# Two-layer trunk on one core: all block sums of the MLPs to VectorE, and their second-half products spread between tiles of the first half

## Chip, cores, metric

One core of a Trainium2 chip. The metric is device time of one execution in microseconds (us); several executions are taken and the median is compared. Engines are named as the profile names them: PE is TensorE (PEld its weight loads), DVE is VectorE, ACT is ScalarE, POOL is GpSimd, SP is SyncE, which here only issues DMAs.

## What is computed

Two layers on 512 tokens of width 1024, all in fp32. Layer 0 mixes tokens by Mamba-2 SSD, layer 1 by HGRN2; each mixer is followed by a layer norm, an MLP of hidden width 4096, a second layer norm and a gated embedding. Cut to the part that is touched:

```python
def sq_relu_mlp(h, w1, w2):
    a = jax.nn.relu(h @ w1)          # [512, 1024] x [1024, 4096]
    return (a * a) @ w2              # [512, 4096] x [4096, 1024]

for i in range(2):
    mix = ssd_mixer(...) if i % 2 == 0 else hgrn2_mixer(...)
    h = layer_norm(ALPHA * x + mix, ...)
    h = layer_norm(ALPHA * h + sq_relu_mlp(h, mlp_w1[i], mlp_w2[i]), ...)
    x = h + sigmoid(h @ ple_w_gate[i]) * (p[i] @ ple_w_proj[i])
```

## The kernel before

**Split products.** Every matrix is held as two halves of fp32r, a rounded one ("hi") and the rest ("lo"), and each product is three matmuls: hi·hi, hi·lo, lo·hi (`mm3`, L116, L117, L118). A weight buffer of 128x1024 comes by one SP DMA of 512 KB into a ring of three (`raws`, L103), ACT casts it to `whi` (L110), DVE subtracts to get `wlo` (L112); the rings of `whi` and `wlo` have five buffers each. This pair of instructions runs for every weight buffer of the kernel, and it is asked for ahead of its use by a priority (`LEAD`).

**First half of an MLP.** A tile is one weight buffer against all tokens: 24 matmuls of 128x512 (rows `pj<-b,whi`). ACT applies Relu and, for two tiles together, Square. Four tiles make a quarter of a hidden group of 8 (`hidden(g, p)`: group g = 0..3, half p = 0, 1). `half_blocks` then makes the seven left operands of a 2x2 Strassen-Winograd product: a11, a12, a22 and four sums s1..s4. Each is split by `put`: ACT cast (L263), DVE subtract (L264). The four sums are POOL instructions (L269 to L275). Operands s3 and s4 lie in the pool `blk` (2 buffers) and the other five in `b8` (9 buffers).

**Second half.** `block_product` of a group is seven products instead of eight: p1 (a11), p2 (a12), p6 (s2), p7 (s3), p5 (s1), p4 (a22), p3 (s4). A product is two halves c = 0, 1 of 12 matmuls, each half into a PSUM bank; at its end DVE adds the bank to `acc` (L314, or L316 for the first group). p1, p6, p5 and p3 all use the same two banks, py0 and py1, one for each c, and keep adding in them: p6's half c can start only when DVE has read p1's half c. The right operands are four weight blocks of two buffers each, and four sums of them, t1..t4: eight buffers come by SP into a ring `r` of ten, and eight POOL instructions make the sums (L290 t1, L292 t2, L321 t3, L325 t4).

**Order.** A scheduler places the instructions of each engine in the order in which they are written, moved forward by the priorities (`LEAD` 100, `SUMS` 220 places). `ORDER` lists quarters of the first half (h, group, half) and whole block products (o): `h00 h01 h10 o0 h11 h20 o1 h21 h30 h31 o2 o3`. So the last two block products of an MLP, 14 products in a row, have no first-half tile between them. In the last one the order of products is p1, p2, p6, p5, p3, then the norm of chunks 0 and 1 (`after`), p7, p4, then chunks 2 and 3.

**Norm.** `norm` takes `acc` by four chunks of 128 tokens: statistics (L189, L191), root (L193), reciprocal (L195), two scalings (L196, L197), and then for each half of the chunk four transpositions on PE (L206) into one bank `pt`, an ACT cast (L209) and a DVE subtract (L210). The norm ahead of the MLP runs between the matmuls of the mixer's output projection and the MLP's first matmuls.

Of the kernel before, what the change touches and what calls it, by code (L numbers as in the profile page):

```python
# [15 lines left out]
P = 128  # L16
T = 512
# [13 lines left out]
ORDER = "h00 h01 h10 o0 h11 h20 o1 h21 h30 h31 o2 o3".split()  # L31
SUMS = 220
# [10 lines left out]
def trunk(ctx: ExitStack, tc, a):  # L43
# [9 lines left out]
    sm = pool("sm", 2)  # L53
    psj = pool("psj", 4, space=PSUM)
# [17 lines left out]
    mlp = dict(r=10, blk=2, sg=2)  # L72
# [67 lines left out]

    begin("ssd")
# [114 lines left out]
    def half_blocks(blk, z0, z1, p):  # L256
# [20 lines left out]

    def block_product(w, blk, first, after=None):


        with tc.high_priority(offset=SUMS):
            raw = {}
            for i, j in ((0, 0), (0, 1), (1, 1), (1, 0)):
                raw[i, j] = []
                for u in range(2):
                    raw[i, j].append(tmp("r", [P, 1024]))
                    nc.sync.dma_start(raw[i, j][u], w[i][j][u])
            t1, t2, t3, t4 = raw[0, 1], [tmp("r", [P, 1024]) for _ in range(2)], raw[0, 0], raw[1, 0]
            for u in range(2):
                nc.gpsimd.tensor_sub(t1[u], raw[0, 1][u], raw[0, 0][u])  # L290
            for u in range(2):
                nc.gpsimd.tensor_sub(t2[u], raw[1, 1][u], t1[u])  # L292
# [3 lines left out]
        def product(x, f, name, start, i, j, then=None):  # L296
            us = [split(v) for v in f]
            if then is not None:
                with tc.high_priority(offset=LEAD):
                    then()  # L300
# [18 lines left out]
        def sums3():  # L319
            for u in range(2):  # L320
                nc.gpsimd.tensor_sub(t3[u], t2[u], raw[0, 0][u])  # L321

        def sums4():
            for u in range(2):
                nc.gpsimd.tensor_sub(t4[u], raw[1, 0][u], t2[u])  # L325

        product("a11", raw[0, 0], "x", True, 0, 0, sums3)
# [6 lines left out]
        if after is None:  # L334
            for f in (p7, p5, p4, p3):
                f()
        else:
            p5(), p3(), after(0), after(1)
            p7(), p4(), after(2), after(3)
# [700 lines left out]
```

## Time and profile before

| | us |
|---|---|
| median of 3 runs (lowest to highest) | 1508.86 (1508.42 to 1509.92) |
| the profiled execution | 1508.68 |
| its span in the trace | 1506.9 |
| PE busy | 1470.1 (98%) |
| DVE busy | 1101.0 (73%) |
| ACT busy | 723.5 (48%) |
| POOL busy | 274.8 (18%) |
| moved by DMA | 149.93 MB, mean 99 GB/s |

Busy time is the sum over the engine's instructions; matmuls overlap, so PE's busy time is not PE at its peak. "Granted clock" is the share of TensorE's full clock in a stretch. In rows of the trace the columns are start, duration, engine, line, operation, output<-inputs, shapes, and in brackets the idle time before the instruction and what ended it. MLP 0 spans about 401 to 727 us of the profiled span, MLP 1 about 1110 to 1436 us.

### The profile page before, as it was taken

To read this page: it belongs to the slowest core of one execution; us is meant where nothing else is said; L and a number is where in the kernel's file an instruction comes from. 1 tells how busy PE (TensorE), PEld (TensorE's weight loads), DVE (VectorE), ACT (ScalarE), POOL (GpSimd) and SP (SyncE) were. 2 spreads that over 40 slices of the span, in tenths; PEclk is the share of its full clock that TensorE was granted. 3 is DMA by queue.
4 is the path that set the end of the run, shared out by engine and by line. 5 is a ranking of instruction groups with operands and counts; after the bars stand their busy time and mean duration, and the time that the engine had idled before them with its cause. 6 is when DMAs were issued, how large, how long until landed. Compare 5 with 4: busy or idle time off the path is not lost.

```text
span 1506.9 us, 19584 instructions
## 1 busy us (share of the span) xinstructions
PE 1470.1 (98%) x7720; PEld 1222.1 (81%) x7720; DVE 1101.0 (73%) x1544; ACT 723.5 (48%) x1020; POOL 274.8 (18%) x136
## 2 busy tenths in 40 slices
PE   8999999999999999998999999999999999999898
PEld 5888888888888888876778998988798888887677
DVE  7998686787777586398944866769766958549883
ACT  6776455563364454453534453543245454444342
POOL 0000000001145251363000000000215435235200
PEclk9999999999999999998999999999999999999999
DMA  6433323234223324130223212222431423314022
GB/s 247 155 112 107 112 93 109 99 118 175 88 69 112 112 89 137 55 126 28 81 70 112 94 61 71 72 70 84 154 112 43 134 90 112 127 42 140 14 85 70
DMA packets 41612, 149.93 MB, mean 99 GB/s; under 512 B 4624, under 2 KB 5136, under 8 KB 41392
## 3 DMA queue, kind: packets, MB, share of 16 engines
q1 hardware_dynamic: 41520, 148.67, 29.4%
q8 instruction: 61, 1.00, 0.3%
q14 instruction: 31, 0.25, 0.1%
HBM read 146.49 MB, written 2.16 MB: 99 GB/s over the span
## 4 chain that ended last, share of the span: by engine, by line
PE 88%; DVE 9%; DMA 2%; ACT 1%; issue 0%; POOL 0%; SPq 0%; ACTq 0%; DVEq 0%
PE pj L116 23%; PE pj L117 23%; PE pj L118 23%; DVE wlo L112 4%; PE py L116 3%; PE py L118 3%; PE py L117 3%; DVE b L264 2%; PE py L778 1%; PE py L587 1%; DVE acc L314 1%; PE pm L557 1%; PE pt L206 1%; PE py L592 1%; DMA a<-in_pT 1%; DVE blk L264 1%
## 5 line engine op out<-in xcount | busy, mean ns | idle before, releaser
L116 PE MATMUL pj<-b,whi 128*128 128x512 f32 (+1 forms) x1024 | 392.0, 383 | 1.2 <-ACT whi L110 1.2
L118 PE MATMUL pj<-b,wlo 128*128 128x512 f32 (+1 forms) x1024 | 388.1, 379 | 0.0
L117 PE MATMUL pj<-b,whi 128*128 128x512 f32 (+1 forms) x1024 | 387.5, 379 | 0.0
L112 DVE TENSOR_TENSOR wlo<-raw,whi 128x1024 fp32r<-128x1024 f32 x180 | 230.4, 1281 | 110.5 <-ACT whi L110 109.6
L110 ACT CAST whi<-raw 128x1024 fp32r<-128x1024 f32 x180 | 188.8, 1050 | 237.3 <-PE pj L117 129.5
L112 DVE TENSOR_TENSOR wlo<-r,whi 128x1024 fp32r<-128x1024 f32 x112 | 194.0, 1737 | 89.7 <-ACT whi L110 89.7
L116 PE MATMUL pj<-whi,b 128*128 128x512 f32 (+1 forms) x712 | 252.3, 355 | 0.5 <-ACT sg L410 0.5
L117 PE MATMUL pj<-wlo,b 128*128 128x512 f32 (+1 forms) x712 | 249.6, 351 | 0.8 <-DVE wlo L112 0.8
L118 PE MATMUL pj<-whi,b 128*128 128x512 f32 (+1 forms) x712 | 250.1, 351 | 0.0
L116 PEld LDWEIGHTS pj<-b,whi 128*128 128x128 f32 x1024 | 192.9, 188 | 36.7 <-ACT whi L110 2.9
L118 PEld LDWEIGHTS pj<-b,wlo 128*128 128x128 f32 x1024 | 192.7, 188 | 35.9 <-DVE wlo L112 1.3
L117 PEld LDWEIGHTS pj<-b,whi 128*128 128x128 f32 x1024 | 192.9, 188 | 34.0 <-issue 1.9
L110 ACT CAST whi<-r 128x1024 fp32r<-128x1024 f32 x112 | 116.8, 1048 | 189.6 <-PE pj L117 60.9
L290 POOL TENSOR_TENSOR r<-r,r 128x1024 f32<-128x1024 f32 x16 | 45.1, 2826 | 767.6 <-DMA r<-in_w 760.0
L117 PEld LDWEIGHTS pj<-wlo,b 128*128 128x128 f32 x712 | 134.7, 189 | 18.4 <-DVE wlo L112 2.0
L116 PEld LDWEIGHTS pj<-whi,b 128*128 128x128 f32 x712 | 134.7, 189 | 17.7 <-ACT sg L410 0.7
L118 PEld LDWEIGHTS pj<-whi,b 128*128 128x128 f32 x712 | 134.5, 189 | 17.0 <-issue 0.2
L116 PE MATMUL py<-whi,b 128*128 128x512 f32 x192 | 77.2, 402 | 15.5 <-DVE acc L314 15.5
L118 PE MATMUL py<-whi,b 128*128 128x512 f32 x224 | 88.8, 398 | 0.0
L264 DVE TENSOR_TENSOR b<-b,b 128x512 fp32r<-128x512 f32 x48 | 62.7, 1322 | 21.5 <-ACT b L263 21.3
L117 PE MATMUL py<-wlo,b 128*128 128x512 f32 x192 | 76.6, 399 | 0.6 <-DVE wlo L112 0.6
L321 POOL TENSOR_TENSOR r<-r,r 128x1024 f32<-128x1024 f32 x16 | 39.8, 2485 | 125.0 <-DVE wlo L112 125.0
(217 smaller groups left out, 2064.3 us busy)
## 6 DMA issues: line engine op xcount, KB each, us to landing
raw<-in_w SPq DMA_DIRECT2D x64, 512.0 KB, 3.6
r<-in_w SPq DMA_DIRECT2D x64, 512.0 KB, 3.7
raw<-in_wssd SPq DMA_DIRECT2D x40, 512.0 KB, 3.6
a<-csd SPq DMA_DIRECT2D x16, 512.0 KB, 3.9
raw<-in_wso SPq DMA_DIRECT2D x16, 512.0 KB, 3.5
raw<-in_wg SPq DMA_DIRECT2D x16, 512.0 KB, 3.6
raw<-in_whvg SPq DMA_DIRECT2D x16, 512.0 KB, 3.5
raw<-in_whq SPq DMA_DIRECT2D x16, 512.0 KB, 3.6
```

The source lines that it names most:

```text
L110: nc.scalar.copy(hi[:, :n], f)
L112: nc.vector.tensor_sub(lo[:, :n], f, f32(hi[:, :n]))
L116: nc.tensor.matmul(out, sh, mh, start=start, stop=False, **kw)
L117: nc.tensor.matmul(out, sh, ml, start=False, stop=False, **kw)
L118: nc.tensor.matmul(out, sl, mh, start=False, stop=stop, **kw)
L206: nc.tensor.transpose(pt[:, j * P : (j + 1) * P], src[:, k * P : (k + 1) * P], ident)
L264: nc.vector.tensor_sub(lo, f, f32(hi))
L290: nc.gpsimd.tensor_sub(t1[u], raw[0, 1][u], raw[0, 0][u])
L314: nc.vector.tensor_add(d, ps, d)
L321: nc.gpsimd.tensor_sub(t3[u], t2[u], raw[0, 0][u])
L557: nc.tensor.matmul(pst_[:, c * P : (c + 1) * P], btok[:, c, :], xw[:, c].rearrange("p h q -> p (h q)"), start=True, stop=True)
L587: nc.tensor.matmul(yd[64 * r : 64 * r + 64, sl], xdt[:, 2 * c + r, :], m[:, r, sl], start=True, stop=True)
```

## The change

All sums go to DVE and are written into the buffer of one of their operands: block sums in `half_blocks` into the activation tiles, weight sums in a new function `weight_sums` into the load buffers. The weight blocks of p1, p2 and p3, which are no sums, are loaded again through the common ring `raws` (`unit` in place of `split`), 6 buffers a group, 48 DMAs of 512 KB in all, so that the ring `r` may be overwritten; `r` has 8 buffers instead of 10. `SUMS` is 300 places instead of 220. The order of the `put`s in `half_blocks` is another. Both `hidden` and `block_product` become generators that stop after each tile (T) and each product (Q), and `PERIODS` interleaves them: eight tiles, then three times fifteen steps in which products of one group alternate with tiles of the next, then the last group's seven products. A tile of 64 bytes per partition is allocated ahead of the phases' pools, which shifts their addresses by 64 bytes.

```diff
-ORDER = "h00 h01 h10 o0 h11 h20 o1 h21 h30 h31 o2 o3".split()
-SUMS = 220
+PERIODS = ("TTTTTTTT",) + 3 * ("TTQTQTQTQTQTQTQ",) + ("QQQQQQQ",)
+SUMS = 300
...
+    pad = pool("pad", 1)
...
-    mlp = dict(r=10, blk=2, sg=2)
+    mlp = dict(r=8, blk=2, sg=2)
...
+    nc.gpsimd.memset(mk(pad, [P, 16], "pad"), 0.0)
...
+        put("a11", a11)
         put("a22", a22)
-        put("a11", a11)
+        nc.vector.tensor_add(a22, a21, a22)
         put("a12", a12)
-        nc.gpsimd.tensor_add(a22, a21, a22)
+        nc.vector.tensor_sub(a21, a11, a21)
+        nc.vector.tensor_sub(a11, a22, a11)
+        nc.vector.tensor_sub(a12, a12, a11)
+        put("s2", a11)
+        put("s3", a21)
         put("s1", a22)
-        nc.gpsimd.tensor_sub(a21, a11, a21)
-        put("s3", a21)
-        nc.gpsimd.tensor_sub(a11, a22, a11)
-        put("s2", a11)
-        nc.gpsimd.tensor_sub(a12, a12, a11)
         put("s4", a12)
...
+    def weight_sums(w):
+
+        t = [[None, None] for _ in range(4)]
+
+        def load(i, u, src):
+            t[i][u] = tmp("r", [P, 1024])
+            nc.sync.dma_start(t[i][u], src)
+
+        with tc.high_priority(offset=SUMS):
+            for u in range(2):
+                load(0, u, w[0][1][u])
+                load(2, u, w[1][1][u])
+                nc.vector.tensor_sub(t[2][u], t[2][u], t[0][u])
+                load(1, u, w[0][0][u])
+                nc.vector.tensor_sub(t[0][u], t[0][u], t[1][u])
+                nc.vector.tensor_add(t[1][u], t[2][u], t[1][u])
+            for u in range(2):
+                load(3, u, w[1][0][u])
+                nc.vector.tensor_sub(t[3][u], t[3][u], t[1][u])
+        return t
...
-            us = [split(v) for v in f]
+            us = [split(v) if f in (t1, t2, t3, t4) else unit(v) for v in f]
...
+        for f in (p1, p2, p6, p5, p3, p7, p4) if after else (p1, p2, p6, p7, p5, p4, p3):
+            f()
+            if after and f is p3:
+                after(0), after(1)
+            if after and f is p4:
+                after(2), after(3)
+            yield
...
+        for g, period in enumerate(PERIODS):
+            if g < 4:
+                tiles = hidden(g)
+            if g > 0:
+                if g == 4:
+                    h_s, after = norm(2 * layer + 1)
+                w = [[[w2[8 * g - 8 + 4 * i + 2 * j + u] for u in range(2)] for j in range(2)] for i in range(2)]
+                products = block_product(w, blocks.pop(g - 1), g == 1, after if g == 4 else None)
+            for op in period:
+                next(tiles if op == "T" else products)
```

Line numbers move with the edit: matmuls from L116-L118 to L117-L119, `whi` and `wlo` from L110 and L112 to L111 and L113, the statistics from L189 and L191 to L191 and L193, the scalings from L196 and L197 to L198 and L199, the norm's subtract from L210 to L212, the addition to `acc` from L314 to L323. In the rows below a name's number is the kernel's own count.

**First place: the start of MLP 0's last group.** DVE's rows before. These rows end products of the group ahead (`py_878` and `py_877` are the shared banks, `pj_5362` and `pj_5363` those of p4) and split the last group's first buffers.

```order
L314 TENSOR_TENSOR acc_94<-py_878_5255,acc_94 128x512
L112 TENSOR_TENSOR wlo_5524<-r_5500,whi_5522 128x1024
L314 TENSOR_TENSOR acc_94<-pj_5362,acc_94 128x512
L112 TENSOR_TENSOR wlo_5528<-r_5502,whi_5526 128x1024
L314 TENSOR_TENSOR acc_94<-pj_5363,acc_94 128x512
L112 TENSOR_TENSOR wlo_5562<-r_5512,whi_5560 128x1024
L314 TENSOR_TENSOR acc_94<-py_877_5254,acc_94 128x512
L112 TENSOR_TENSOR wlo_5566<-r_5514,whi_5564 128x1024
```

POOL's rows before, the weight sums of that last group: t1, t2, then t3 written into the buffers `r_5500` and `r_5502` that two of the DVE rows above read, and t4 into `r_5512` and `r_5514` that the other two read.

```order
L290 TENSOR_TENSOR r_5504<-r_5504,r_5500 128x1024
L290 TENSOR_TENSOR r_5506<-r_5506,r_5502 128x1024
L292 TENSOR_TENSOR r_5516<-r_5508,r_5504 128x1024
L292 TENSOR_TENSOR r_5517<-r_5510,r_5506 128x1024
L321 TENSOR_TENSOR r_5500<-r_5516,r_5500 128x1024
L321 TENSOR_TENSOR r_5502<-r_5517,r_5502 128x1024
L325 TENSOR_TENSOR r_5512<-r_5512,r_5516 128x1024
L325 TENSOR_TENSOR r_5514<-r_5514,r_5517 128x1024
```

DVE's rows now at the same place. `py_860` is the last bank of the group ahead, `py_940` and `py_941` are p1's halves c = 0 and 1 of the last group, `pj_5611` is p2's first half. POOL has nothing left here.

```order
L323 TENSOR_TENSOR acc_99<-py_860_5050,acc_99 128x512
L323 TENSOR_TENSOR acc_99<-py_940_5571,acc_99 128x512
L113 TENSOR_TENSOR wlo_5645<-r_5549,whi_5643 128x1024
L323 TENSOR_TENSOR acc_99<-pj_5611,acc_99 128x512
L191 BN_STATS lnst_5745<-acc_99 128x6
L113 TENSOR_TENSOR wlo_5675<-r_5535,whi_5673 128x1024
L113 TENSOR_TENSOR wlo_5679<-r_5544,whi_5677 128x1024
L113 TENSOR_TENSOR wlo_5711<-raw_5707,whi_5709 128x1024
L323 TENSOR_TENSOR acc_99<-py_941_5572,acc_99 128x512
```

The weight sums of this group stand earlier in DVE's row now, and the addition that frees p1's second bank stands behind three `wlo` rows.

PE's rows before, the end of p1's first half (`py_927`) and the beginning of its second (`py_928`); `pj_5570` is p2's first half.

```order
L116 MATMUL py_927_5532<-whi_5526,b_820_4915 128x512
L117 MATMUL py_927_5532<-wlo_5528,b_820_4915 128x512
L118 MATMUL py_927_5532<-whi_5526,b_820_4915 128x512
L116 MATMUL pj_5570<-whi_5560,b_821_4916 128x512
L116 MATMUL py_928_5533<-whi_5522,b_820_4915 128x512
L117 MATMUL py_928_5533<-wlo_5524,b_820_4915 128x512
L118 MATMUL py_928_5533<-whi_5522,b_820_4915 128x512
```

PE's rows now: `py_941` is p1's second half, `pj_5612` the second half of p2, `py_940` the first half of p6.

```order
L117 MATMUL pj_5612<-whi_5607,b_830_4941 128x512
L117 MATMUL py_941_5572<-whi_5561,b_829_4940 128x512
L118 MATMUL py_941_5572<-wlo_5563,b_829_4940 128x512
...
L119 MATMUL py_941_5572<-whi_5567,b_829_4940 128x512
L118 MATMUL pj_5612<-wlo_5609,b_830_4941 128x512
L119 MATMUL pj_5612<-whi_5607,b_830_4941 128x512
L117 MATMUL py_940_5571<-whi_5639,b_833_4944 128x512
```

p1's second half stood ahead of all but one matmul of p2 and now stands behind 22 of p2's 24, two matmuls ahead of p6's first half.

**Second place: the last chunk of the norm ahead of MLP 0.** DVE's rows before, from the second statistics to the first subtract of the transposed half.

```order
L189 BN_STATS lnst_3329<-acc_94 128x6 x2
L112 TENSOR_TENSOR wlo_3617<-raw_3613,whi_3615 128x1024
L191 BN_AGGR lnmv_3332<-lnst_3329 128x2
L196 SCALAR_TENSOR_TENSOR acc_94<-acc_94,lnmv_3332,a_3098 128x1024
L195 RECIPROCAL lnrs_3336<-lnsd_3334 128x1
L197 SCALAR_TENSOR_TENSOR acc_94<-acc_94,lnrs_3336,b_3099 128x1024
L210 TENSOR_TENSOR b_555_3104<-pt_3340,b_553_3102 128x4x128
```

DVE's rows now; rows L292 to L298 are weight sums of group 0.

```order
L191 BN_STATS lnst_3334<-acc_99 128x6 x2
L292 TENSOR_TENSOR r_3850<-r_3850,r_3848 128x1024
L212 TENSOR_TENSOR b_557_3110<-pt_3299,b_555_3108 128x4x128
L193 BN_AGGR lnmv_3337<-lnst_3334 128x2
L294 TENSOR_TENSOR r_3848<-r_3848,r_3853 128x1024
L197 RECIPROCAL lnrs_3341<-lnsd_3339 128x1
L198 SCALAR_TENSOR_TENSOR acc_99<-acc_99,lnmv_3337,a_3103 128x1024
L295 TENSOR_TENSOR r_3853<-r_3850,r_3853 128x1024
L199 SCALAR_TENSOR_TENSOR acc_99<-acc_99,lnrs_3341,b_3104 128x1024
L298 TENSOR_TENSOR r_3857<-r_3857,r_3844 128x1024
L298 TENSOR_TENSOR r_3860<-r_3860,r_3853 128x1024
L212 TENSOR_TENSOR b_556_3109<-pt_3345,b_554_3107 128x4x128
```

Five weight sums and a subtract of the chunk before have come into this stretch, and a `wlo` has gone out of it.

More of the change, by code (lines that the diff above doesn't have):

```diff
@@ L293, in block_product, with product @@
+    def block_product(w, blk, first, after=None):
+        t1, t2, t3, t4 = weight_sums(w)
         seen = set() if first else {(i, j) for i in range(2) for j in range(2)}
         banks = {}
-        def product(x, f, name, start, i, j, then=None):
-            us = [split(v) for v in f]
-            if then is not None:
-                with tc.high_priority(offset=LEAD):
-                    then()
+        def product(x, f, name, start, i, j):
+            us = [split(v) if f in (t1, t2, t3, t4) else unit(v) for v in f]
@@ L317, in product @@
             seen.add((i, j))
[L319 to L327, printed above, removed]
-        product("a12", raw[1, 0], "z", True, 0, 0, sums4)
-        product("s2", t2, "x", False, 1, 0)
+        p1 = lambda: product("a11", w[0][0], "x", True, 0, 0)
+        p2 = lambda: product("a12", w[1][0], "z", True, 0, 0)
+        p6 = lambda: product("s2", t2, "x", False, 1, 0)
         p7 = lambda: product("s3", t3, "y", True, 1, 1)
```

85 lines of the change are left out of this document (31 added, 54 removed).

## Prediction
> **What bounds the kernel now.** I read the busy shares first, then PE's waits, then the trace around the longest of them.
>
> ```profile
> PE 1470.1 (98%) x7720; PEld 1222.1 (81%) x7720; DVE 1101.0 (73%) x1544; ACT 723.5 (48%) x1020; POOL 274.8 (18%) x136
> PE py L116 <- DVE acc L314: 15.5, 5, 6.3
> PE pt L206 <- DVE acc L197: 3.3, 2, 1.8
> PE pj L117 <- DVE wlo L112: 4.4, 4, 1.8
> ```
>
> PE is busy 98% of the span, and the change takes no matmul away. What it can win is time in which PE stands or runs at a lower clock. PE's waits (total, times, longest) name one large one: a product on the shared banks waits for DVE's addition to `acc`. Its place:
>
> ```profile
> 684.56 0.39 PE L118 MATMUL py<-whi,blk 128*128 128x512 f32 x1
> 683.46 2.39 POOL L321 TENSOR_TENSOR r<-r,r 128x1024 f32<-128x1024 f32 x1 [1.23 <-DVE wlo L112]
> 683.84 3.09 DVE L112 TENSOR_TENSOR wlo<-r,whi 128x1024 fp32r<-128x1024 f32 x1
> 686.85 0.68 DVE L314 TENSOR_TENSOR acc<-pj,acc 128x512 f32<-128x512 f32 x1
> 687.07 2.34 POOL L321 TENSOR_TENSOR r<-r,r 128x1024 f32<-128x1024 f32 x1 [1.23 <-DVE wlo L112]
> 687.45 3.04 DVE L112 TENSOR_TENSOR wlo<-r,whi 128x1024 fp32r<-128x1024 f32 x1
> 690.42 0.68 DVE L314 TENSOR_TENSOR acc<-py,acc 128x512 f32<-128x512 f32 x1
> 691.24 0.77 PE L116 MATMUL py<-whi,b 128*128 128x512 f32 x1 [6.29 <-DVE acc L314]
> 702.59 1.22 DVE L112 TENSOR_TENSOR wlo<-r,whi 128x1024 fp32r<-128x1024 f32 x1
> 703.73 0.68 DVE L314 TENSOR_TENSOR acc<-pj,acc 128x512 f32<-128x512 f32 x1
> ```
>
> Here, at the start of MLP 0's last group, POOL makes the weight sums of that group while DVE makes `wlo`. The two take turns, and a `wlo` lasts 3.0 to 3.1 us; the same instruction with POOL idle lasts 1.22 and lets the next start after 1.14 (702.59 to 703.73). An addition, short of a second anyway, stays at 0.68. DVE falls behind, and PE stands 6.29 us. The clock then tells the rest (window, then busy time of PE, PEld, DVE, ACT, POOL, granted clock, DMA share, GB/s):
>
> ```profile
> 660.00:665.00 5.00, 3.22 (x11) 2.27 (x10) 5.00 (x5) 1.89 (x3) 2.68 (x1) 0.82 0.51 185
> 685.00:690.00 5.00, 0.00 (x0) 0.00 (x0) 5.00 (x3) 2.07 (x3) 3.19 (x2) 0.71 0.00 0
> 690.00:695.00 5.00, 3.76 (x9) 3.02 (x10) 5.00 (x5) 0.00 (x0) 3.27 (x2) 0.50 0.01 3
> 1370.00:1375.00 5.00, 4.00 (x17) 3.12 (x17) 5.00 (x4) 1.32 (x2) 3.19 (x2) 1.00 0.32 105
> ```
>
> After the stall PE comes back at half clock (0.50). Two shorter stalls lie ahead of it and of its twin in MLP 1, alike in length and not in effect:
>
> ```profile
> 662.63 0.50 PE L117 MATMUL pj<-wlo,blk 128*128 128x512 f32 x1 [1.78 <-DVE wlo L112]
> 1371.01 0.50 PE L117 MATMUL pj<-wlo,blk 128*128 128x512 f32 x1 [1.77 <-DVE wlo L112]
> ```
>
> **The loss to be had.** I measure it over the whole run of products without a tile between, by three starts of matmuls for the pace and by the starts of its first matmul and of the first transposition behind it.
>
> ```profile
> 654.75 0.39 PE L118 MATMUL py<-whi,b 128*128 128x512 f32 x1
> 658.83 0.39 PE L118 MATMUL py<-whi,b 128*128 128x512 f32 x1
> 659.06 0.40 PE L116 MATMUL pj<-whi,blk 128*128 128x512 f32 x1
> 679.19 0.40 PE L116 MATMUL py<-whi,blk 128*128 128x512 f32 x1
> 727.25 0.60 PE L206 MATMUL pt<-cst,acc 128*128 128x128 f32 x4
> 1367.44 0.40 PE L116 MATMUL pj<-whi,blk 128*128 128x512 f32 x1
> 1435.61 0.60 PE L206 MATMUL pt<-cst,acc 128*128 128x128 f32 x4
> ```
>
> From 654.75 to 658.83 are 18 matmuls, 0.2267 us each. From 679.19 to 684.56 (quoted above) are 23 of a product whose operand lies in `blk`, 0.2335 each: 6.7 ns more. Between 659.06 and 727.25 PE does 236 matmuls, 48 of them from `blk`; at these paces 53.6 us. It takes 68.19, so 14.6 us are lost: 6.3 and 1.8 of standing, the rest half clock and short waits. MLP 1: 68.17 us, 14.5 lost. Together 29.1 us.
>
> **The change part by part.**
>
> *Sums off POOL.* POOL keeps memsets only, so no `wlo` waits its turn. The groups (busy, mean ns, then idle) and the landing of a load (KB, us):
>
> ```profile
> L112 DVE TENSOR_TENSOR wlo<-r,whi 128x1024 fp32r<-128x1024 f32 x112 | 194.0, 1737 | 89.7 <-ACT whi L110 89.7
> L112 DVE TENSOR_TENSOR wlo<-raw,whi 128x1024 fp32r<-128x1024 f32 x57 | 69.4, 1218 | 21.8 <-ACT whi L110 21.8
> L110 ACT CAST whi<-r 128x1024 fp32r<-128x1024 f32 x112 | 116.8, 1048 | 189.6 <-PE pj L117 60.9
> L290 POOL TENSOR_TENSOR r<-r,r 128x1024 f32<-128x1024 f32 x16 | 45.1, 2826 | 767.6 <-DMA r<-in_w 760.0
> L264 DVE TENSOR_TENSOR b<-b,b 128x512 fp32r<-128x512 f32 x48 | 62.7, 1322 | 21.5 <-ACT b L263 21.3
> r<-in_w SPq DMA_DIRECT2D x64, 512.0 KB, 3.7
> ```
>
> DVE gets back 112 x (1.74 - 1.22) = 58 us on `wlo` of `r` and 48 x (1.32 - 0.68) = 31 on splits of blocks, and pays 64 weight sums and 64 block sums. The trace has no such sum on DVE; a `wlo` is also a 128x1024 subtract of two buffers, so I take 1.14 and, for the half as large block sum, 0.60: 73 + 38 us. The ends are 0.5 us below (no gain is excluded) and POOL's 2.83 above; the row on the same engine is the nearest. DVE's busy time so stays near 1.12 ms.
>
> *Interleaving.* Of the 14 products in a row 7 now have a tile between each two. In a period of 15 steps of 24 matmuls, 15 x 24 x 0.2267 = 82 us of PE, DVE has 22 `wlo` (8 tiles, 14 product buffers), 8 weight sums at 1.14, 14 additions, 14 splits and 8 block sums at 0.60: 56 us. ACT has 22 casts of 1.05 and the block casts, under 45. The reserve is some 25 us a period, so the whole 29.1 us goes: **-29.1**.
>
> *Loads.* 48 DMAs of 512 KB more (25 MB on 149.93) and a row of SP that may wait for one of eight `r` buffers ahead of `raw` loads. Five split buffers stand between a load and its use, each worth 2.7 to 5.4 us of PE, more than 8 us against a landing of 3.7. I cost them at nothing; if that cover went, a 3.7 us landing at a period's start would come out, and up to six of them (22 us) in the worst case.
>
> *The last seven products.* They still run without tiles, at 7 x 24 matmuls to 14 splits, 14 additions and the norm's rows, which DVE holds by itself. But p1's second half stands now 22 matmuls later on PE. By hand, from the end of the first half of the last product ahead (0): PE needs 2.72 for the second half, 2.72 for p1's first, 5.0 for 22 of p2, so p1's second half runs 10.65 to 13.4. DVE has 13 short rows and 2 long until the addition that frees that bank, 13 x 0.60 + 2 x 1.14 = 10.1, done at 10.5: no wait. p1's first split buffer is free after six of those matmuls, at 12.2; ACT's cast into it (1.05) and `wlo_5645` (1.22) end at 14.5. Queued behind them on DVE are an addition (0.60), the statistics (0.65) and three `wlo` (3.4), and only then comes the addition of `py_941`, done at 19.8. p6's first half ends at 16.55. PE stands 3.35 us, with restart 3.6; both MLPs: **+7.2**. The ends: 0 (if the three `wlo` fall into an earlier gap) and 2 x 6.3, the stall of before.
>
> *The norm ahead of the MLPs.*
>
> ```profile
> 376.12 2.49 DVE L196 SCALAR_TENSOR_TENSOR acc<-acc,lnmv,a 128x1024 f32<-128x1024 f32 x1
> 379.85 2.09 DVE L197 SCALAR_TENSOR_TENSOR acc<-acc,lnrs,b 128x1024 f32<-128x1024 f32 x1
> 382.08 0.63 PE L206 MATMUL pt<-cst,acc 128*128 128x128 f32 x4 [1.84 <-DVE acc L197]
> 398.15 1.28 DVE L197 SCALAR_TENSOR_TENSOR acc<-acc,lnrs,b 128x1024 f32<-128x1024 f32 x1
> 400.87 0.69 DVE L210 TENSOR_TENSOR b<-pt,b 128x512 fp32r<-128x512 f32 x1 [1.43 <-ACT b L209]
> 401.61 0.66 PE L206 MATMUL pt<-cst,acc 128*128 128x128 f32 x4
> ```
>
> Eight sums of group 0 fall into DVE's row here. Between the last chunk's statistics and its last scaling stand three sums and a subtract more and a `wlo` less, 3 x 1.14 + 0.60 - 1.14 = 2.9, less some 0.5 since the slowed scalings of 2.49 and 2.09 go back to 1.28 and the 1.84 us stall goes: the scaling ends at 401.85 instead of 399.43. Two sums ahead of the next subtract, 2.3 us where DVE had 1.43 idle, add 0.7. The last transposition starts at 404.7 instead of 401.61, less 0.24 for two short matmuls done before it: +2.9. In MLP 1 the sums fall mostly earlier in the norm; the same walk gives +0.7. Together **+3.6**, ends 0 and 9.1 (all eight sums on the path in one of the two).
>
> *Half clock.* A window at half clock of about 3.4 us costs 1.7. Both stalls of 6.3 were followed by one, and the 1.78 at 662.63 (0.82), not the 1.77 at 1371.01 (1.00) nor the 1.84 at 382.08. The changed kernel has by the above two of 3.4, one of 3.0 and some of 1.4: I take one and a half windows, **+2.6**; ends 0 and 6. The Trainium skill has a rule for this in "TensorE: Matmul & The Clock Gate", section "HAM oscillation — how this bites in real kernels": gaps in PE's work of more than about 3.4 us bring the half clock. By that rule none of the new stalls would, and the sum would be the one of rival C below; the 6.3 us stalls agree with it, the 0.82 after 1.78 us does not.
>
> *64 bytes.* `blk` is the one operand of these that lies in the phases' pool, which the padding shifts; 384 matmuls of it x 6.7 ns = 2.6 us. What sets this pace no row tells. I take that the shift brings `blk` to `b8`'s pace, **-2.6**; ends -2.6 and +2.7 (other phases' operands move the other way).
>
> Sum against the profiled execution, which at 1508.68 is 0.2 below the median of 1508.86: 1508.7 - 29.1 + 7.2 + 3.6 + 2.6 - 2.6 = 1490.4, so **1490**.
>
> **Rivals.**
>
> *B, half of the last run's stall stays.* The last group is still seven products without tiles, and DVE is busy in every window quoted above around the stall; if its row of 15 ahead of the last group is late by more than my 0.15 us of reserve, each MLP loses another 3.7 (half of the 6.3 with a share of half clock): 1490.4 + 7.4 = 1497.8. Against it: no instruction there is slowed by POOL any more. 0.20.
>
> *C, no stall of the new kernel halves the clock.* The longest is 3.4 us by my count, about half of the two that were followed by it, and of the trace's three below 1.9 us two were harmless: 1490.4 - 2.6 = 1487.8. Against it: 1.78 us sufficed at 662.63, so the length alone does not decide. 0.20.
>
> *D, the other side: DVE's bunches at the period boundaries starve PE.* At each boundary the second `half_blocks` of a group (7 splits and 4 sums, 6.6 us) and rows of the next weight sums stand between two additions on the shared banks, 10.5 us by the order; PE needs the bank after 16.3, so 5.8 are spare. There are six boundaries. The gain of 18.3 is gone when each costs 3.1, so when a bunch is 8.9 us longer, nearly double; with POOL's 2.83 for each of its sums it would be. At 4 us each: 1514. 0.06.
>
> *E, the stall is not POOL's doing, or comes back with the sums on DVE.* If DVE's reserve is an illusion because sums of two buffers cost as much there as on POOL, nothing is won: 1509. Against it speak 1.22 against 3.09 in the same loop. 0.04.
>
> **How the numbers follow.** My forecast has 0.45, with a range of its own from 1484 to 1496 (the clock and `blk` ends); 0.05 is left for something better, the late wait of the last group missing (1483). The range for 8 in 10 takes in B and C with their own 3 or 4 us, 1480 to 1504. A measurement of this kernel can tell about 0.2%, 3 us: faster than 1505.8 are all but D and E, 0.90; within 0.2% E, 0.04; slower D, 0.06.
>
> **What would show it.** POOL's busy time under 3 us, no `wlo` above 1.3 us, DVE busy near 1.12 ms. The longest wait of PE on the additions 3 to 4 us instead of 6.3, at p6's second half in the last group, and a new wait for the last transposition ahead of MLP 0 of about 3. No wait above 1 us inside the periods. Products of `blk` at 0.227 a matmul. I am wrong if PE waits for DVE at a period's boundary, if loads of `raw` come late behind waiting loads of `r`, or if a stretch of half clock lies where PE never stood.

## The result, and the profile after

The changed kernel takes 1490.43 us (median of 4 runs, 1487.04 to 1492.68) against 1509.39 before (1508.42 to 1513.29): a ratio of 0.9868, 95% interval 0.9841 to 0.9894, so 1.3% faster. The forecast was 1490. The profiled execution is the fastest of the four, 1487.04 us with a span of 1485.3. All lines of after in this section are from it.

Busy time on the page, and the groups of `wlo` (busy, mean ns, idle before):

```profile
PE 1463.3 (99%) x7720; PEld 1219.7 (82%) x7720; DVE 1086.6 (73%) x1672; ACT 725.3 (49%) x1020; POOL 0.9 (0%) x9
L113 DVE TENSOR_TENSOR wlo<-raw,whi 128x1024 fp32r<-128x1024 f32 x228 | 278.5, 1222 | 154.8 <-ACT whi L111 153.9
L113 DVE TENSOR_TENSOR wlo<-r,whi 128x1024 fp32r<-128x1024 f32 x64 | 78.1, 1221 | 31.8 <-ACT whi L111 31.7
```

POOL is empty but for the memsets, every `wlo` takes 1.22 us, and DVE with 128 sums more is less busy than before (1086.6 against 1101.0). Of PE's waits (total, times, longest) these are the ones that lie in the norms and the MLPs; larger are two that the kernel before has too, for its first weights (4.3, before 4.2) and in a gate (2.6, before 2.2).

```profile
PE pt L208 <- DVE acc L199: 2.6, 2, 2.4
PE py L117 <- DVE acc L323: 1.9, 2, 1.0
PE pj L117 <- ACT b L211: 1.3, 2, 0.7
PE pt L208 <- DVE b L212: 1.3, 3, 0.7
```

The 15.5 us of waiting for additions are 1.9 now, and among these waits the norm has taken the first place. At the start of MLP 0's last group DVE and PE show this:

```profile
691.29 1.29 DVE L323 TENSOR_TENSOR acc<-py,acc 128x512 f32<-128x512 f32 x2
692.49 1.22 DVE L113 TENSOR_TENSOR wlo<-r,whi 128x1024 fp32r<-128x1024 f32 x1
693.62 0.69 DVE L323 TENSOR_TENSOR acc<-pj,acc 128x512 f32<-128x512 f32 x1
694.35 0.69 DVE L191 BATCH_NORM_STATS2 lnst<-acc 128x6 f32<-128x512 f32 x1
694.96 2.44 DVE L113 TENSOR_TENSOR wlo<-r,whi 128x1024 fp32r<-128x1024 f32 x2
697.32 1.22 DVE L113 TENSOR_TENSOR wlo<-raw,whi 128x1024 fp32r<-128x1024 f32 x1
698.45 0.68 DVE L323 TENSOR_TENSOR acc<-py,acc 128x512 f32<-128x512 f32 x1
699.19 0.50 PE L117 MATMUL py<-whi,b 128*128 128x512 f32 x1 [0.97 <-DVE acc L323]
```

These are the rows that the prediction named, in the order it named: the addition of p1's second bank stands behind three `wlo`, and p6's second half waits for it. It waits 0.97 us and not 3.35.

Where the 21.6 us of span went is read best by stretches between starts of transpositions, which PE does in the same order in all kernels here: the norm (from the first transposition of the norm ahead of an MLP to the first of its last four), the MLP (from there to the first transposition of the norm behind), and what is between.

| stretch, us | before | after | difference |
|---|---|---|---|
| to the first norm | 372.96 | 372.83 | -0.13 |
| norm ahead of MLP 0 | 28.65 | 31.45 | +2.80 |
| MLP 0 | 325.63 | 313.45 | -12.18 |
| gate 0 and HGRN2 | 354.67 | 355.05 | +0.38 |
| norm ahead of MLP 1 | 27.84 | 28.72 | +0.88 |
| MLP 1 | 325.85 | 312.49 | -13.36 |

### The profile page after: what moved, and what is told of

The parts are those of the page before. It is cut to its first block, busy times and chain, and to the rows that moved or that the text cites. A ratio compares the mean times of both kernels' runs of the same rounds, so it can differ in the third digit from the quotient of the medians.

```text
span 1485.3 us, 19598 instructions
## 1 busy us (share of the span) xinstructions
PE 1463.3 (99%) x7720; PEld 1219.7 (82%) x7720; DVE 1086.6 (73%) x1672; ACT 725.3 (49%) x1020; POOL 0.9 (0%) x9
## 2 busy tenths in 40 slices
DMA packets 48526, 175.10 MB, mean 118 GB/s; under 512 B 5393, under 2 KB 5905, under 8 KB 48305
## 4 chain that ended last, share of the span: by engine, by line
PE 92%; DVE 6%; DMA 1%; ACT 1%; issue 1%; SPq 0%; ACTq 0%
PE pj L117 24%; PE pj L118 23%; PE pj L119 23%; PE py L117 4%; PE py L118 4%; PE py L119 4%; DVE wlo L113 2%; PE py L784 1%; PE py L593 1%; PE pm L563 1%; PE py L598 1%; PE pt L208 1%; PE py L794 1%; PE py L829 1%; ACT whi L111 1%
## 5 line engine op out<-in xcount | busy, mean ns | idle before, releaser
L111 ACT CAST whi<-raw 128x1024 fp32r<-128x1024 f32 x228 | 239.1, 1049 | 329.6 <-PE pj L118 176.0
L117 PE MATMUL pj<-b,whi 128*128 128x512 f32 (+1 forms) x1024 | 391.4, 384 | 3.0 <-ACT whi L111 1.6
L113 DVE TENSOR_TENSOR wlo<-raw,whi 128x1024 fp32r<-128x1024 f32 x228 | 278.5, 1222 | 154.8 <-ACT whi L111 153.9
L118 PE MATMUL pj<-b,whi 128*128 128x512 f32 (+1 forms) x1024 | 387.7, 379 | 0.0
L119 PE MATMUL pj<-b,wlo 128*128 128x512 f32 (+1 forms) x1024 | 387.6, 379 | 0.0
L117 PE MATMUL pj<-whi,b 128*128 128x512 f32 (+1 forms) x712 | 252.0, 355 | 0.5 <-ACT sg L416 0.5
L118 PE MATMUL pj<-wlo,b 128*128 128x512 f32 (+1 forms) x712 | 249.8, 351 | 0.8 <-DVE wlo L113 0.8
L119 PE MATMUL pj<-whi,b 128*128 128x512 f32 (+1 forms) x712 | 249.8, 351 | 0.0
L117 PEld LDWEIGHTS pj<-b,whi 128*128 128x128 f32 x1024 | 192.9, 189 | 38.9 <-ACT whi L111 3.0
L119 PEld LDWEIGHTS pj<-b,wlo 128*128 128x128 f32 x1024 | 193.0, 189 | 35.7 <-DVE wlo L113 1.2
L118 PEld LDWEIGHTS pj<-b,whi 128*128 128x128 f32 x1024 | 193.2, 189 | 33.9 <-issue 1.9
L118 PEld LDWEIGHTS pj<-wlo,b 128*128 128x128 f32 x712 | 134.7, 189 | 18.2 <-DVE wlo L113 2.0
L117 PEld LDWEIGHTS pj<-whi,b 128*128 128x128 f32 x712 | 134.6, 189 | 17.8 <-ACT sg L416 0.7
L119 PEld LDWEIGHTS pj<-whi,b 128*128 128x128 f32 x712 | 134.6, 189 | 17.0 <-issue 0.2
L111 ACT CAST whi<-r 128x1024 fp32r<-128x1024 f32 x64 | 67.1, 1049 | 113.6 <-PE pj L118 90.9
L113 DVE TENSOR_TENSOR wlo<-r,whi 128x1024 fp32r<-128x1024 f32 x64 | 78.1, 1221 | 31.8 <-ACT whi L111 31.7
L119 PE MATMUL py<-whi,b 128*128 128x512 f32 x224 | 87.1, 390 | 0.0
L117 PE MATMUL py<-whi,b 128*128 128x512 f32 x192 | 75.1, 391 | 1.9 <-DVE acc L323 1.9
L118 PE MATMUL py<-wlo,b 128*128 128x512 f32 x192 | 74.7, 389 | 0.0
L498 DVE SCALAR_TENSOR_TENSOR cv<-pj,cst,cv 128x511 f32<-128x511 f32 (+2 forms) x72 | 53.3, 744 | 5.8 <-ACT cv L495 5.2
L119 PEld LDWEIGHTS py<-whi,b 128*128 128x128 f32 x224 | 42.0, 188 | 8.9 <-DVE b L394 0.3
L117 PEld LDWEIGHTS py<-whi,b 128*128 128x128 f32 x192 | 36.0, 188 | 10.7 <-DVE acc L323 3.3
```

Source lines behind the costliest of these rows:

```text
L111: nc.scalar.copy(hi[:, :n], f)
L113: nc.vector.tensor_sub(lo[:, :n], f, f32(hi[:, :n]))
L117: nc.tensor.matmul(out, sh, mh, start=start, stop=False, **kw)
L118: nc.tensor.matmul(out, sh, ml, start=False, stop=False, **kw)
L119: nc.tensor.matmul(out, sl, mh, start=False, stop=stop, **kw)
L498: nc.vector.scalar_tensor_tensor(cv[:, d:], ps[:, : T - d], convw[:, i, k : k + 1], cv[:, d:], ALU.mult, ALU.add)
```

## Experiments

The comparisons of each group of runs have runs of the kernel before on the same chip beside them; its median in them was 1512.4 to 1514.5 us. Ratios are against it, with 95% intervals. The times are medians; the four stretches, in us, are those of one execution each, and stretches of half clock can make them differ by some 1.7 us from one execution to the next.

| kernel | us | ratio | norm 0 | MLP 0 | norm 1 | MLP 1 |
|---|---|---|---|---|---|---|
| before | | 1 | 28.65 | 325.63 | 27.84 | 325.85 |
| changed, again | 1491.2 | 0.9861 [0.9840, 0.9883] | 31.45 | 315.20 | 28.71 | 312.54 |
| without padding | 1492.4 | 0.9858 [0.9845, 0.9872] | 31.44 | 315.37 | 28.71 | 314.16 |
| changed, old order | 1518.5 | 1.0036 [1.0024, 1.0048] | 31.45 | 328.09 | 28.71 | 326.39 |
| changed, last period alone interleaved | 1504.8 | 0.9940 [0.9927, 0.9954] | 31.46 | 321.42 | 28.71 | 319.80 |
| changed, all sums on POOL | 1512.1 | 0.9994 [0.9983, 1.0005] | 35.63 | 316.94 | 37.24 | 318.12 |
| before, block sums on DVE | 1503.2 | 0.9936 [0.9922, 0.9951] | 28.67 | 322.22 | 27.84 | 320.52 |
| first sums held | 1482.0 | 0.9799 [0.9780, 0.9817] | 26.72 | 312.83 | 26.15 | 313.15 |
| held, later weight sums doubled | 1481.1 | 0.9781 [0.9768, 0.9794] | 26.52 | 312.84 | 26.15 | 313.11 |
| held, p2 ahead of p1 | 1483.0 | 0.9793 [0.9780, 0.9806] | 26.63 | 313.41 | 26.14 | 313.70 |
| held, weight sums on POOL | 1481.2 | 0.9789 [0.9772, 0.9806] | 26.53 | 313.05 | 26.16 | 313.10 |
| held, block sums on POOL | 1490.9 | 0.9852 [0.9836, 0.9867] | 26.57 | 317.87 | 26.15 | 317.06 |
| held, all sums on POOL | 1494.6 | 0.9879 [0.9862, 0.9897] | 26.69 | 318.84 | 26.17 | 322.34 |

**The changed kernel once more.**

> The changed kernel once more, for a second trace and for its spread. Theory: the steps of the order repeat to 0.1 us (first transposition of MLP 0's last norm 313.4 us after the last one of the norm ahead, waits of 0.97 us at p6 and 2.41 us ahead of the last chunk), and what differs between executions is only the granted clock: a time of 1487 with no stretch under full clock, 1.5 to 2 us more for each stretch of half clock in the trace. Rival: the spread comes from DMA landings or waits that move from execution to execution; then waits of PE differ by more than 0.5 us between the two traces at a full clock.

1491.2 us, and the waits repeat: 2.4 us in the norm, 1.0 at p6. What differs in the trace from the first one is two places. From the first matmuls to 13 us it is 1.9 us later, and behind the norm it loses 1.7 us. There the granted clock stands in windows of 3 us (PE, PEld, DVE, ACT, POOL, clock, DMA, GB/s), first in the execution of 1487, where the norm's last transposition starts at 404.28:

```profile
403.00:406.00 3.00, 2.64 (x12) 2.35 (x12) 2.36 (x3) 0.57 (x1) 0.00 (x0) 0.50 0.02 5
406.00:409.00 3.00, 3.00 (x26) 3.00 (x25) 0.69 (x1) 0.36 (x2) 0.00 (x0) 0.94 0.54 175
409.00:412.00 3.00, 3.00 (x27) 3.00 (x27) 1.23 (x1) 1.86 (x3) 0.00 (x0) 1.00 0.03 7
```

then in this one, where it starts at 406.17:

```profile
403.00:406.00 3.00, 1.40 (x8) 0.95 (x8) 3.00 (x4) 0.59 (x1) 0.00 (x0) 0.88 0.00 0
406.00:409.00 3.00, 2.83 (x14) 2.84 (x14) 1.94 (x3) 0.59 (x1) 0.00 (x0) 0.50 0.23 49
409.00:412.00 3.00, 3.00 (x16) 3.00 (x16) 0.00 (x0) 0.00 (x0) 0.00 (x0) 0.50 0.33 131
```

Both fall to half clock at the norm's last waits. The first is back when the long row of matmuls begins; in the second some 6 us at half clock cover 30 of them. So the 2.4 us wait has a price of its own and at times 1.7 us behind it. At the kernel's start the same four matmuls of `wdt` read, in the first trace and in this one:

```profile
9.72 1.05 PE L440 MATMUL pj<-acc,raw 128*32 128x512 f32 x4
```

```profile
10.65 1.92 PE L440 MATMUL pj<-acc,raw 128*32 128x512 f32 x4
```

Twice as long, for some 3 us, and then the pitch is alike: half speed here too, though the windows of the profile have 1.00. The trace's own record of the clock shows why: its first entry, at full clock, lies at 7.00 us in the first trace and at 12.74 us in this one, and the slow matmuls of this one end there (from 12.94 on they start 0.23 us apart). The theory holds for both places.

The records show more. In all 14 traces the clock changes only at distances that are multiples of 3.413 us. So each trace can be cut into windows of that length, and what PE did in one can be set against the clock in the next. Here are two windows of before, with the 1.78 and the 1.77 us wait that the prediction found alike in length and not in effect, then two of the first trace and one of the second around the norm's last wait (columns as above):

```profile
659.79:663.20 3.41, 1.63 (x7) 1.02 (x6) 3.41 (x5) 2.10 (x3) 1.07 (x1) 1.00 0.38 148
1369.76:1373.17 3.41, 2.17 (x9) 1.80 (x10) 3.41 (x3) 0.51 (x1) 2.71 (x1) 1.00 0.34 103
```

```profile
399.53:402.94 3.41, 0.77 (x5) 0.56 (x6) 3.41 (x4) 0.58 (x1) 0.00 (x0) 1.00 0.00 0
402.94:406.36 3.42, 3.06 (x14) 2.77 (x15) 2.73 (x4) 0.59 (x1) 0.00 (x0) 0.50 0.02 5
```

```profile
405.28:408.69 3.41, 2.70 (x14) 2.53 (x13) 2.66 (x4) 0.59 (x1) 0.00 (x0) 0.50 0.15 24
```

The wait of 1.78 us lies whole in its window and leaves PE 1.63 of 3.41 us busy: half clock follows. Of the wait of 1.77 us 1.25 lie in the window, PE is busy for 2.17, and none follows. Over all traces, full clock was lost behind every window in which PE was busy for less than 0.46 of it and behind none with more than 0.54; in between both occur. From half clock it came back behind windows with 0.84 and more (3.06 of 3.42 in the first trace), and not behind those with 0.79 and less (2.70 of 3.41 in the second). So where a wait lies against the windows decides with its length, and that differs between executions.

The Trainium skill says in "TensorE: Matmul & The Clock Gate", section "What's actually happening", that the gate looks at a window of about 3.4 us that runs free of the kernel, so that the number of slow matmuls at a start differs from execution to execution. The two rows of the start and the 3.413 us of the records agree with it.

**Sums on DVE, old order.** One line:

```diff
-PERIODS = ("TTTTTTTT",) + 3 * ("TTQTQTQTQTQTQTQ",) + ("QQQQQQQ",)
+PERIODS = ("TTTTTTTT",) + 2 * ("TTTTQQQQQQQTTTT",) + ("TTTTTTTTQQQQQQQ", "QQQQQQQ")
```

> All sums on DVE as changed, but tiles and products in the order of before (four tiles, seven products, four tiles; the last 14 products in a row). If the sums' move off POOL is what takes the stall away, 1488 to 1496: in the 14 products DVE has 2 x 1.14 + 2 x 0.60 for a product and 9.1 us of sums over seven, 4.8 of each 5.44 us, so short waits of 1 to 2 us may show and no 6.3. If the interleaving is what does it, the stall of some 6 us in each MLP stays with its half clock, and the time is 1500 to 1510.

1518.5 us, slower than before by 0.36%. Both theories had the stall no longer than before; it is longer. The wait in PE's list, and DVE's and PE's rows around one of the two:

```profile
PE py L117 <- DVE acc L323: 22.7, 4, 11.3
669.19 0.68 DVE L323 TENSOR_TENSOR acc<-py,acc 128x512 f32<-128x512 f32 x1
...
673.26 1.22 DVE L292 TENSOR_TENSOR r<-r,r 128x1024 f32<-128x1024 f32 x1
674.39 1.22 DVE L113 TENSOR_TENSOR wlo<-r,whi 128x1024 fp32r<-128x1024 f32 x1
675.53 1.22 DVE L294 TENSOR_TENSOR r<-r,r 128x1024 f32<-128x1024 f32 x1
676.66 0.69 DVE L323 TENSOR_TENSOR acc<-pj,acc 128x512 f32<-128x512 f32 x1
677.26 1.22 DVE L295 TENSOR_TENSOR r<-r,r 128x1024 f32<-128x1024 f32 x1
678.40 2.41 DVE L298 TENSOR_TENSOR r<-r,r 128x1024 f32<-128x1024 f32 x2
...
682.45 1.28 DVE L323 TENSOR_TENSOR acc<-py,acc 128x512 f32<-128x512 f32 x2
683.28 0.77 PE L117 MATMUL py<-whi,b 128*128 128x512 f32 x1 [10.30 <-DVE acc L323]
```

No row is slow: each 128x1024 subtract takes 1.22. But between two additions of the shared banks (669.19 and 682.45) stand 12.7 us of other rows, five of them weight sums for the next group, and PE has nothing else to do. The count of the expectation, 4.8 us of DVE in 5.44 of PE, says nothing of the order within.

**Interleaving in the last period alone.** The first two periods as in the old order.

> The changed kernel with the old order in the first two periods (four tiles, seven products, four tiles) and the interleaved one in the third alone. If the whole gain lies where 14 products stood in a row, the time is that of the changed kernel within 2 us (1487 to 1493) and no wait is over 1 us in the first two periods. If DVE with its sums needs the interleaving everywhere, seven products in a row with the next group's sums among them starve PE as in the old order, some 2 to 11 us a period, and the time is 1495 to 1515.

1504.8 us: not the first theory. Where seven products of the second period stand in a row, PE waits 5.25 us for an addition (at 571.68) and comes back at half clock; DVE's rows there are full from 554 to 574 with sums, splits and `wlo`. MLP 1 has the same wait (5.24 us at 1275.60). The first and the third period have none like it.

```profile
571.68 0.77 PE L117 MATMUL py<-whi,b 128*128 128x512 f32 x1 [5.25 <-DVE acc L323]
```

**All sums on POOL, new order.** `nc.vector` becomes `nc.gpsimd` in the eight lines of sums.

> The changed order and buffers, but all block sums and weight sums on POOL. If the sums' move is what counts, a wlo is 1.6 us or more on the mean, DVE is late at the periods' boundaries and in the last group, and the time is 1500 to 1515; the norm ahead of the MLPs gets back its 3.7 us. If the interleaving is what counts, POOL's 34 us a period (8 x 2.6 and 8 x 1.6) are hidden beside 42 us of DVE in 82, and the time is 1488 to 1496.

1512.1 us, no change against before, and both theories were half right: the time is in the range of the first, but the norms, which were to get their 3.7 us back, lose more. The two MLPs are 16.4 us shorter than before, so the new order hides most of what POOL's sums cost there; at p6 PE still waits 3.6 us in each. The norms are 16.4 us longer: all eight sums of group 0 run in them now, and slow the chunks' scalings, which PE waits for:

```profile
388.70 6.67 POOL L298 TENSOR_TENSOR r<-r,r 128x1024 f32<-128x1024 f32 x2
389.83 3.33 DVE L198 SCALAR_TENSOR_TENSOR acc<-acc,lnmv,a 128x1024 f32<-128x1024 f32 x1
393.68 2.77 DVE L199 SCALAR_TENSOR_TENSOR acc<-acc,lnrs,b 128x1024 f32<-128x1024 f32 x1
396.59 1.09 PE L208 MATMUL pt<-cst,acc 128*128 128x128 f32 x4 [5.35 <-DVE acc L199]
```

A scaling takes 1.28 with POOL idle.

**Holding the first sums.** The load of the first operand of group 0's sums has to wait for a one-column copy out of the norm's last result, so the sums can't run before the norm is done.

```diff
+            if hold is not None and i == 0:
+                nc.vector.tensor_copy(t[i][u][:, 0:1], hold)
...
+                hold = f32(h_s.lo[1])[:, 3, 511:512] if g == 1 else None
```

> The changed kernel, with the first two weight loads of each MLP's first group held back until the norm's last subtract is done (a one-column DVE copy into the load buffer), so that the eight sums fall behind the norm. If the sums in the norm cost 2.8 and 0.9 us, as the traces of before and after show, and DVE's idle time in the first tiles (3.0, 1.5, 1.0 us at 407 to 415) takes them, 3 to 5 us less than the changed kernel. Rival: the sums then delay the first tiles' wlo or p6, and nothing or less than 1 us is won.

1482.0 us, 9 less than the changed kernel in the same comparison, and more than expected. The norms shrink by 4.7 and 2.6 us, 7.3 together, where I had counted from before's norms, which themselves lost 1.9 and 1.7 to POOL's sums. The rest is the half clock behind the norm, which is gone with the waits. No wait for a transposition of the norm is left in PE's list, of which these are the rows behind the first weights:

```profile
PE pt L429 <- DVE acc L423: 2.4, 2, 1.5
PE py L117 <- DVE acc L325: 1.9, 2, 1.0
PE pj L118 <- DVE wlo L113: 0.8, 2, 0.4
```

(L429 belongs to the gate.) The sums run from 407 to 420 us among the first tiles, and MLP 0 is no longer for it (312.83 against 313.45).

**Later weight sums doubled.** On the held kernel, for each weight sum of groups 1 to 3 one more is made close behind it, into a buffer that nothing reads.

> The kernel that holds the first weight sums behind the norm (1482), with every later weight sum doubled by a sum of the same size into a buffer that nothing reads: 48 more DVE instructions of 1.14 us, 9.1 us in each period. If a period has a reserve of some 20 us of DVE, as counted in the prediction, the time stays within 2 us, 1480 to 1485. If it is the place of the sums among the additions and not the mean load that decides, as the 11 us stall of the old order suggests, PE waits at a boundary or in the last group and the time is 1487 to 1500.

1481.1 us: the 55 us of DVE work cost nothing that can be measured, and the longest wait for an addition stays at 1.0. A period has at least 9 us of DVE to spare.

**p2 ahead of p1.** In the last group of the held kernel, `(p2, p1, p6, p5, p3, p7, p4)`.

> The kernel that holds the first weight sums behind the norm, with p2 ahead of p1 in the last group, so that PE has 24 matmuls on other banks while DVE frees the shared ones, and p1's second half stands right behind its first. If the 0.97 us wait at p6 and the interleaved halves around it (1.4 us an MLP over the pace) come from that order, 2 to 3 us less than 1482 and no wait of PE for an addition over 0.3 us. Rival: the addition of p1's bank is late anyhow because DVE makes its splits for p6 and p5 there, and the wait only moves; then 1481 to 1483.

1483.0 us, the same; each MLP is about 0.6 us longer. The wait moved and grew (1.7 us at longest): the rival was right.

**Which sums.** On the held kernel, sums go back to POOL by kind.

> As the held kernel, with the block sums alone on POOL. The 3.57 us wait at p6 in the kernel with all sums on POOL has a chain of four block sums before it on POOL (688.77 to 696.09) and splits of 1.5 to 2.3 us on DVE beside them; no weight sum is near. If the block sums make that wait, it is here too: 3 to 4 us in each last group and half clock in some, 1487 to 1491. If they do not, 1481 to 1483.

> As the held kernel, with the weight sums alone on POOL. If the reserve of a period covers slowed wlo rows (eight sums of 2.4 to 3.3 us, each costing DVE about as much), PE waits nowhere for them but in the first group, behind the norm: 1481 to 1485. If the weight sums are what hurts with POOL, 1487 or more and a wait of PE for an addition or a wlo of over 2 us inside the periods.

> The kernel that holds the first weight sums behind the norm, with all sums on POOL: the interleaving alone, without the damage to the norm that the kernel with all sums on POOL took (7.0 and 9.4 us). If the parts add, the two MLP stretches are those of that kernel, 316.9 and 318.1 us against 312.8 and 313.1 with DVE's sums, and the norms those of the held kernel (26.7 and 26.2): 1482 + 9 = 1491. If the interleaving needs the sums on DVE, the MLPs grow by 6 us or more each (eight POOL sums of 2.4 to 3.3 us now beside the first tiles) and the time is over 1495.

Weight sums on POOL: 1481.2 us, no loss. `wlo` of `r` is slowed there as it was before, and no wait comes of it:

```profile
PE py L117 <- DVE acc L325: 1.9, 2, 1.0
L113 DVE TENSOR_TENSOR wlo<-r,whi 128x1024 fp32r<-128x1024 f32 x64 | 106.6, 1673 | 27.5 <-ACT whi L111 27.4
```

Block sums on POOL: 1490.9 us, and the wait at p6 is there. POOL's chain of four, the `wlo` and splits beside it, and PE:

```profile
680.14 1.67 POOL L270 TENSOR_TENSOR b<-a,b 128x512 f32<-128x512 f32 x1 [35.57 <-DVE b L266]
681.90 2.15 POOL L272 TENSOR_TENSOR a<-a 128x512 f32<-128x512 f32 x1
684.13 1.62 POOL L273 TENSOR_TENSOR a<-b,a 128x512 f32<-128x512 f32 x1
685.83 1.63 POOL L274 TENSOR_TENSOR b<-b,a 128x512 f32<-128x512 f32 x1
686.22 2.31 DVE L113 TENSOR_TENSOR wlo<-r,whi 128x1024 fp32r<-128x1024 f32 x1
690.99 0.79 PE L117 MATMUL py<-whi,b 128*128 128x512 f32 x1 [3.55 <-DVE acc L325]
```

The last split can't start before the last of four sums, at 687.5, and the addition stands behind it; behind this wait and its twin in MLP 1 half clock follows. All on POOL with the sums held: 1494.6, above the 1491 that adding the parts gave, and the MLPs are 6.0 and 9.2 us longer than the held kernel's (in an execution of 1498.1). Beside the same two waits PE waits 1.94 us for a `whi` among MLP 1's first tiles (at 1138.55), where POOL's sums now stand, and half clock follows. The new order with the sums held, and all of them on POOL, so is worth 1.2%; 3.6 us of that are the norms.

**The kernel before with the block sums on DVE.**

> The kernel before, with the four block sums alone on DVE (same order, weight sums still on POOL). If the 6.3 us stall of the last 14 products belongs to the weight sums that POOL makes beside wlo, as the rows around it show, it stays, and the time is that of before within 3 us. If DVE's backlog there begins with the block sums and their slowed splits, the stall falls under 4 us in each MLP, its half clock with it, and the time is 5 to 12 us less than before.

1503.2 us, 0.64% faster than before. The longest wait is nearly halved, the total falls by a quarter (before: 15.5 in total, 6.3 at longest):

```profile
PE py L116 <- DVE acc L314: 11.8, 6, 3.5
```

So the block sums have their part in the stall that the prediction read from the weight sums alone: with them on DVE the MLPs are 3.4 and 5.3 us shorter. Half clock still follows, for 6.8 us in each MLP, where before has 13.7 in MLP 0 and 6.8 in MLP 1.

**Without the padding.** The two lines with `pad` taken out.

> The changed kernel without the 64 bytes of padding. The prediction took the padding to bring matmuls of the operands in blk from 0.2335 to 0.2267 us; the trace of after has them at 0.2327. If the padding made that small difference, they are at 0.2335 here, 0.3 us in all, and the time is that of the changed kernel, 1487 to 1493. If the padding has a use elsewhere, another phase is longer by 1 us or more, seen at the anchors of the transpositions.

The time is the changed kernel's (0.9858 against 0.9861). Matmuls of `blk` have a pitch of 0.2334 us here and 0.2327 with the padding: 0.7 ns, 0.3 us over 384 of them. No other phase moved. Behind MLP 0's norm stand 6.8 us at half clock, as in the second trace of the changed kernel; MLP 1 is 1.6 us longer than there, with 3.4 us at half clock behind its norm, where the waits are 0.7 us as they are there.

## Why the prediction came out, and where it did not

| term, us | predicted | measured |
|---|---|---|
| stall of the last 14 products | -29.1 | -28.1 |
| p6 in the last group | +7.2 | +2.8 |
| sums in the norms | +3.6 | +3.7 |
| half clock | +2.6 | 0 in the profiled execution, 1.7 in the second, with 1.9 at the kernel's start |
| padding | -2.6 | -0.3 |

The measured terms with 0.3 of small differences add up to -21.6 us, the difference of the two spans. The median is 3.4 us above the profiled execution. So the time of 1490 was met in part by luck: two errors of 4.4 and 2.3 us in opposite directions, and the half clock that came and went, nearly cancelled.

*The stall.* Its size was a little high: of the 236 matmuls 92 and not 48 are from `blk`, which makes 54.1 us of them and 14.1 lost in each MLP (and with 48 the prediction's own paces make 53.8 us, not 53.6). That all of it goes was right. The reason was only part of it. The last link of before's stall was read rightly, though the block sums have their part in it. The last addition to a shared bank ahead of the one that PE waited for (at 690.42) is this:

```profile
679.62 0.68 DVE L314 TENSOR_TENSOR acc<-py,acc 128x512 f32<-128x512 f32 x1
680.22 3.10 DVE L112 TENSOR_TENSOR wlo<-r,whi 128x1024 fp32r<-128x1024 f32 x1
```

Between the two lie 10.2 us, most of them three `wlo` slowed to 3.0 to 3.1 us. What the gain comes from is another question. The prediction took the sums' leaving POOL for the cause, with the interleaving as reserve. The parts by themselves, on the sum of both MLP stretches against before: interleaving with all sums on POOL -16.4 us (-10.3 with the first sums held, which puts them back into the MLPs), block sums alone on DVE -8.7, all sums on DVE without interleaving +3.0, everything -25.5. With the interleaving, weight sums may run on either engine (1482.0 and 1481.2 us), but block sums on POOL cost 8.9 us (1490.9). Without interleaving, with the changed kernel's ring, loads and `SUMS`, all sums on DVE make the wait 11 us instead of 6; which of these gathers the rows into one burst was not taken apart. So the step that failed is "POOL keeps memsets only, so no `wlo` waits its turn" as the source of the gain: in the changed order, with the first sums held, a mean `wlo` of 1.67 us costs nothing, and in the old order a `wlo` of 1.22 does not help. What the rows of these kernels have in common is that the time of DVE's rows between two additions of the shared banks counts, while PE has nothing but products. A tile between two products brings one `wlo` and no addition, and so 5.4 us of PE in which DVE can catch up; the doubled sums show that this reserve is there. DVE's busy time was forecast near 1.12 ms and is 1.087: more rows than those counted had been slowed by POOL, among them `wlo` of `raw` (1281 ns on the mean before, 1222 now).

*The last group.* The order was read rightly and the wait found where it was said. The term was too large because the cast ahead of `wlo_5645` was taken to wait for a split buffer of p1. In the trace ACT starts it at 691.33, after a matmul of p2 let it go, and `wlo` runs at 692.49, 11.0 us after the prediction's zero (681.5) and not 13.3. So the additions come 2.3 us earlier, and the wait is 1.0. Beside it 0.4 us an MLP go in switches between half products.

*The norm.* Met in the sum, 3.6 against 3.7, and within 0.4 us in the place: the last transpositions of MLP 0's norm start at 404.28 us, against 404.7. What was missed is that sums in the norm cost before as well, on POOL. Against a norm without any sums the change costs 4.7 and 2.6 us, and the held kernel shows that DVE has room for them right behind it.

*The clock.* "One and a half windows" was a guess. The traces show half clock around the norm's wait of 2.4 us and the two of 0.7 after it: 3.4 us of it in the profiled execution, while PE had little to do, and 6.8 us in the second. Two executions of the same rows differ by 1.7 us in that. The two waits at p6, on which the prediction counted too, are 1.0 us and have none behind them. The rule of rival C, the Trainium skill's in "TensorE: Matmul & The Clock Gate", section "HAM oscillation — how this bites in real kernels", would have no half clock after gaps below about 3.4 us; these rows are against it as a bound. Rival C had the profiled execution's time (1487.8) and lacked the spread.

*Rivals.* B did not come: the row ahead of the last group was in time. D did not come in this order, but its mechanism is real and larger than its price in the prediction: in the old order with DVE's sums, 12.7 us of rows between two additions cost 10.3 us at one place. E did not come: a sum on DVE costs 1.22 us, as a `wlo` does.

*Loads.* 48 DMAs more are in the trace (175.10 MB against 149.93) and PE waits for none of them, as costed.

*Padding.* It was taken for the reason of `blk`'s slower pace because nothing else in the diff had to do with it; the trace gave the pace and no cause. The run without it gives 0.3 us.

The best kernels here are the one with the first sums held (1482.0) and its twin with weight sums on POOL (1481.2), 2.0% and 2.1% under before; the two do not differ beyond their intervals.

## To carry to other kernels

Where an engine serves a pipeline, count the time of its rows between the two that free a shared buffer, not its mean load: 12.7 us of rows at no more than 1.2 us each made PE wait 10.3 us, and 10.2 us with three rows of 3.1 made it wait 6.3. Work of another kind put between the critical steps gives a reserve. With it, it no longer mattered here which engine makes the weight sums, but it did for the block sums, which stand in a chain of four ahead of the last splits. Work that a scheduler can start early it will start early, into the next latency-bound stage too; tie it to the end of that stage.

## What the runs showed of the chip

Two 128x1024 subtracts of two buffers on DVE start 1.14 us apart, and with a POOL sum beside them one lasts up to 3.1; a scaling with one more operand goes from 1.28 to 3.33. Half clock came with the norm's wait of 2.4 us and the two of 0.7 behind it in each of the five traces that have them, for 3.4 or 6.8 us. The clock changed only at multiples of 3.413 us: it fell behind windows of that length in which PE was busy for about half of the time or less (always under 0.46, never over 0.54), and came back behind windows with 0.84 or more. A shift of the buffers by 64 bytes changed the pitch of `blk`'s matmuls by 0.7 ns in 233; no other effect of it was seen.
